# Attention kernel: 22 units' probabilities and B's values transposed as the rounded 32-bit type, one unit on

## The chip, the cores and the metric

The kernel runs on one NeuronCore of a Trainium2 chip. Its engines are TensorE (PE, with its weight load shown apart as PEld), VectorE (DVE), ScalarE (ACT), GpSimd (POOL) and SyncE (SP, which here only issues transfers). Each engine runs its own instructions in their order and waits on semaphores for the others. The metric is the device time of one execution in microseconds (us).

## The reference

One layer of an encoder on 1024 tokens of width 1024, in float32: a half-step FFN, then a mixer of two attentions, then a second half-step FFN. The mixer is what matters here:

```
u = RMSNorm(h)
qA,kA,vA,qB,kB,vB,gA,gB = split(u @ W_in)
yA = NeighbourhoodAttention2D(qA, kA, vA)        # 8 heads, 8x16 window, learned bias
yB = WindowedGQA(rope(qB), rope(kB), vB)         # 8 heads, 2 key heads, |i-j| <= 128, sink logit
h = h + (sigmoid(gA) * (yA @ W_A) + sigmoid(gB) * (yB @ W_B)) @ W_out
```

Both attentions are a softmax of scores over a band of keys, p = exp(s - max) / sum, and then p @ v.

## The kernel before

All large products are done on TensorE with both factors split in two tiles of the rounded 32-bit type (`fp32r` in the profile, `F32R` in the code): a high part, and the rest. Three matmuls (lines 149, 153 and 155, function `mm3`) make one product. The FFNs, the input projection and the branch products all go through `mm3`; the weights and activations are split by ACT (a cast, the high part) and DVE (a subtraction, the low part), mostly in `split`, lines 95 and 98.

Between them stands the attention stage, of some 230 us (from about 917 to 1160 us of the span). It handles 64 **units**, one after the other: a unit is a block of 128 queries with two heads. The first 32 are B's (`units_b`: eight blocks j, four pairs of heads each), the last 32 A's. A unit has nk = 3 blocks of 128 keys, in the first and the last block of queries only 2. Four functions make the steps of a unit, and the loop at the end of the stage lays them out as a pipeline, one unit entering per round n:

- `scores` (round n): on PE four matmuls into two PSUM tiles "d" (lines 1596 and 1597), then on DVE a custom operation that adds the mask or bias and keeps the running maximum (L1601), then on ACT the exponential with its sum (L1604). The result, the unscaled probabilities, lies in the tile `fa` in two places used in turn for two units of three, and in two `held` tiles (`hs` in the profile) for every third unit.
- `scale` (one round later): a reciprocal on DVE (L1610), and the scaling of one head on DVE (L1611) and of the other on ACT (L1612), in place.
- `turn` (two rounds later): nk transposes on PE for each of the two heads, 128 x 128 each, with the identity `ident`, into PSUM tiles "d" (L1620); then `split` of each (ACT L95, DVE L98) into tiles `ws`.
- `values` (three rounds later): on PE the products with the values (L1639 for B, L1634 for A), into a PSUM tile "g"; then the write, for B an ACT copy (L1539) and a DVE addition (L1540).

Between these steps the loop puts pieces of other PE work, the **filler**: first the products of the gates (`gate`, six matmuls of 512 columns in `mm3` for one piece, with ACT copies L1331 at the end of each gate), then B's branch products. The gates' weights come by SP transfers `ws<-wg_d` (L1228, 512 KB each, two per gate). A's operands come by POOL transfers (`prep_a`, L1303, L1306).

B's values are made earlier: `v_b` (L1153 to L1156) loads a row block of `z_d` by an SP transfer, and `turn_v` transposes it, eight transposes of 128 x 128 (L1163), before they are split.

What sets the order: outside the hand-written first stage, a list scheduler reorders the instructions of all engines by its own estimate of their times, so the order on each engine is not that of the code. The ring `raw` has four buffers of 512 KB, `ws` eight, the PSUM tags "d" and "g" four banks each.

Of the kernel before, what the change touches and what calls it, by code (L numbers as in the profile page):

```python
# [9 lines left out]

F32 = mybir.dt.float32
# [4 lines left out]
P = 128  # L16
# [15 lines left out]
def f32v(ap):  # L32
    return ap.bitcast(F32)
# [3 lines left out]
def trunk_kernel(ctx, tc, x, xt, n1, wg1, wu1, wd1, nm, win, rpb, sink, wa, wb, wout,  # L37
# [17 lines left out]
        uid[0] += 1  # L55
        return f"{s}_{uid[0]}"

    ident = const.tile([P, P], F32, name="ident")
    make_identity(nc, ident)
    nhalf4 = const.tile([P, 4], F32, name="nhalf")  # L60
    nc.gpsimd.memset(nhalf4, -0.5)
    nhalf = nhalf4[:, 0:1]
# [74 lines left out]
    def turned(xs):  # L137
        pts = []
        for half in range(2):
            pt = bank("d")  # L140
            for c in range(4):
                nc.tensor.transpose(pt[:, c * P:(c + 1) * P], xs[:, (half * 4 + c) * P:(half * 4 + c + 1) * P], ident)  # L142
            pts.append(pt.rearrange("p (c t) -> p c t", c=4))
        return pts

# [768 lines left out]
    def keep_busy(n):  # L914

        b = bank("g")
        for i in range(n):
            k = i % 4 * P
            nc.tensor.transpose(b[:, k:k + P], ident, ident)

    def first_stage():
        load, _, _, _, pieces, (multiply, finish), hand_over, load_early = hg
# [39 lines left out]
        def do(op, a):  # L962
# [13 lines left out]
            elif op == "eps":  # L976
                i = int(a[0])
                nc.vector.tensor_scalar(st[i][1], st[1][0] if i else mean[0].rearrange("p (k c) -> p k c", c=P)[:, :, 0], EPS, None, op0=ALU.add)
            elif op == "pow":
                i = int(a[0])  # L980
                nc.gpsimd.tensor_tensor(st[i][0], st[i][1], nhalf4, op=ALU.pow)
            elif op == "spread":
                i = int(a[0])
                r[i] = bank("d" if i else "g")
                for k in range(4):
                    nc.tensor.transpose(r[i][:, k * P:(k + 1) * P], st[i][0][:, k:k + 1].to_broadcast([P, P]), ident)
            elif op == "stat":
                t = int(a[0])
                nc.scalar.activation(toks[:, t - 4], toks[:, t - 4], AF.Square, scale=D ** -0.5,
                                     accum_out=st[1][0][:, t - 4:t - 3])  # L990
            elif op == "keep":
                rms["row"] = main.tile([P, 512], F32, tag="s1", bufs=1, name=nm_("s1"))
                nc.scalar.copy(rms["row"], r[0])
            elif a[0] == "X":
                c = int(a[1])
                h, l = [v[:, c, :] for v in rhs(B21)]
                if op == "hi":
                    nc.scalar.activation(h, block(c, 0, 1), AF.Copy, scale=n1c[:, 4 + c:5 + c])
                else:
                    nc.vector.scalar_tensor_tensor(out=l, in0=block(c, 0, 1), scalar=n1c[:, 4 + c:5 + c], in1=f32v(h),  # L1000
                                                   op0=ALU.mult, op1=ALU.subtract)
            elif op == "y":
                n, h, c = int(a[0][0]) - 1, int(a[0][1]) - 1, int(a[1])
                d, k = block(c, h, n), 4 * n + c
                nc.vector.scalar_tensor_tensor(out=d, in0=d, scalar=n1c[:, k:k + 1],
                                               in1=rms["row"] if (n, h) == (1, 0) else r[h], op0=ALU.mult, op1=ALU.mult)
            elif op == "t":
                c = int(a[1])
                y11, y21, y12, y22 = block(c, 0, 0), block(c, 0, 1), block(c, 1, 0), block(c, 1, 1)
                d, u, v = {"1": (y12, y12, y11), "2": (y22, y22, y12), "3": (y11, y22, y11), "4": (y21, y21, y22)}[a[0]]  # L1010
                nc.vector.tensor_tensor(d, u, v, op=ALU.subtract)
            elif a[0] in RIGHTS:
                c = int(a[1])
                src, g = block(c, *BLOCKS[a[0]]), RIGHTS[a[0]]
                if ar[g].dtype != F32R:
                    new_ar(g)
                h, l = [v[:, c, :] for v in rhs(RIGHTS[a[0]])]
                if op == "hi":
                    nc.scalar.copy(h, src)
                else:  # L1020
                    nc.vector.tensor_tensor(l, src, f32v(h), op=ALU.subtract)
            elif op == "load":
                i, m, half = [int(k) for k in a]
                load(i, m, half, {(0, 0): 4, (0, 1): 5, (1, 0): 6}[m, half])
            else:
                q = int(a[1]), a[0], int(a[2])
                if op == "mm":
                    if q not in mm:
                        mm[q] = multiply(*q)
                    drain(mm[q], 1)  # L1030
                elif op == "x":
                    drain(finish(*q), 1)
                else:
                    if q not in pc:
                        pc[q] = pieces(*q)
                    pc[q].pop(op)()
# [115 lines left out]

    def v_b():  # L1153
        mix["vb"] = [new_fx(k, F32R).rearrange("p (t d) -> p t d", t=NTT) for k in (0, 1)]
        mix["vr"] = xs4()
        pin(nc.sync.dma_start(mix["vr"], z_d[17 * P:18 * P, :]))  # L1156

    def turn_v():
        r = mix["vr"]
        for n in range(2):  # L1160
            pt = bank("g")
            for i in range(4):
                nc.tensor.transpose(pt[:, i * P:(i + 1) * P], r[:, (4 * n + i) * P:(4 * n + i + 1) * P], ident)  # L1163
            pt = pt.rearrange("p (b s d) -> p b s d", s=2, d=HD)
            for s in range(2):
                v = mix["vb"][s][:, 4 * n:4 * n + 4, :]
                split(v[:, :, :HD], v[:, :, HD:], pt[:, :, s, :])
# [410 lines left out]
                           bias=[bias_at(hp, s, edge) for s in range(2)], sink=None, write=write)  # L1578

    npair = [0]  # L1580

    def scores(un):
        j = un["j"]
# [2 lines left out]
        moff = (k0 - j + 1) * P  # L1586
        ext = 0 if un["sink"] is None else 1
        nmx, ssum, rc = small("nmx"), small("ssum"), small("rc")
        un.update(k0=k0, nk=k1 - k0, pr=[], ssum=ssum, rc=rc)
        third = npair[0] % 3 == 2  # L1590
        both = None if third else fa[:, 1536 + 2 * (npair[0] % 3) * (384 + ext):][:, :2 * (384 + ext)].rearrange("p (s k) -> p s k", s=2)
        if ext and not third:
# [1 line left out]
        for s in range(2):  # L1594
# [8 lines left out]
                                           accum_out=nmx[:, s:s + 1])  # L1603
            nc.scalar.activation(pr, pr, AF.Exp, scale=-1.0, bias=nmx[:, s:s + 1], accum_out=ssum[:, s:s + 1])  # L1604
            un["pr"].append(pr[:, ext:])
        npair[0] += 1

    def scale(un):
        rc = un["rc"]
        nc.vector.reciprocal(rc, un["ssum"])  # L1610
        nc.vector.tensor_scalar_mul(un["pr"][0], un["pr"][0], rc[:, 0:1])  # L1611
        nc.scalar.activation(un["pr"][1], un["pr"][1], AF.Copy, scale=rc[:, 1:2])  # L1612

    def turn(un):
        nk = un["nk"]
        un["p"] = [ws4()[:, :768].rearrange("p (k s t) -> p k s t", k=3, s=2) for _ in range(2)]
        for s in range(2):
            pt = bank("d")
            for i in range(nk):
                nc.tensor.transpose(pt[:, i * P:(i + 1) * P], un["pr"][s][:, i * P:(i + 1) * P], ident)  # L1620
            if len(un["v"]) == 2:
                dst = [un["p"][s][:, :nk, k, :] for k in range(2)]
            else:
# [34 lines left out]
    for n in range(1 << 30):  # L1658
# [9 lines left out]
        if prep:  # L1668
            drain(prep, 1)
        filling(n)  # L1670
        if len(pipe) > 2 and pipe[2] is not None:
            turn(pipe[2])
        if prep:
            drain(prep, 1)
        if n >= 26 and (n - 26) % 8 == 0 and n < 58:
# [8 lines left out]
        if n == 63:  # L1684
            form("P2", 0, mix["ya", 2][:, L])
        filling(n)
        if len(pipe) > 3 and pipe[3] is not None:
            values(pipe[3])
        pipe = pipe[:4]
        if not any(pipe):  # L1690
            break
    drain(fill)

# [247 lines left out]
```

## Time and profile before

| | us |
|---|---|
| median of 3 runs | 1912.72 (1911.67 to 1912.93) |
| the profiled execution | 1912.05 |
| its span | 1910.1 |
| PE busy in the span | 1901.1 (100%) |
| DVE busy | 1456.1 (76%) |
| ACT busy | 961.3 (50%) |

The profile is of one execution. The span runs from the first to the last instruction; the 1.95 us beside it lie around it. In the groups of instructions a row gives line, engine, operation, tiles, shape and count, then busy time, mean duration of one in ns, and the idle time of the engine just ahead of them. The duration of one matmul is longer than the distance to the next, because they are pipelined: the distance is read from the chain of waits, where a row gives start, time and what, and x6 means six in a row. A row with "issue" is time in which the engine waited for nothing that the profile shows.

### The profile page before, as it was taken

Reading aid. Unit: us, or ns where it says so; the run is one execution under the profiler, and the core shown is the slowest. Engines: PE = TensorE matmul, PEld = TensorE weight load, DVE = VectorE, ACT = ScalarE, POOL = GpSimd, SP = SyncE. Lnnn points to the kernel's source line nnn. Section 1 sums busy time; section 2 is a strip of 40 time slices with the busy share of each in tenths; the row PEclk is TensorE's granted clock in tenths of the full one; section 3 lists DMA queues with packets and bytes.
Section 4 is the critical chain, followed back from the end, with each engine's and each line's share of the span. In section 5 each row is a group of like instructions: output and inputs, shape, how many; then the busy total and the mean of one; then the engine's idle time right before and its main releaser. Section 6 shows DMA issues by size and latency. Waiting matters only on the chain.

```text
span 1910.1 us, 26150 instructions
## 1 busy us (share of the span) xinstructions
PE 1901.1 (100%) x9020; PEld 1595.1 (84%) x9020; DVE 1456.1 (76%) x2644; ACT 961.3 (50%) x1876; POOL 244.3 (13%) x453
## 2 busy tenths in 40 slices
PE   9999999999999999999999999999999999999998
PEld 8888888888888888898898888888888888888886
DVE  8988888868957788666888999789665566559664
ACT  7533545544446543444898885274333333344453
POOL 0011232210000112211112300010010001000011
PEclk9999999999999999999999999999999999999999
DMA  7256977887454367855647969653333323492341
GB/s 270 95 188 217 336 273 289 298 293 282 127 166 135 112 206 225 243 192 206 181 123 207 296 227 335 232 195 132 136 111 107 108 89 111 162 357 93 110 139 61
DMA packets 176963, 365.84 MB, mean 192 GB/s; under 512 B 17728, under 2 KB 75968, under 8 KB 176832
## 3 DMA queue, kind: packets, MB, share of 16 engines
q1 hardware_dynamic: 136784, 236.23, 37.6%
q0 software_dynamic: 39184, 126.90, 19.2%
q8 instruction: 71, 1.16, 0.3%
q10 hardware_dynamic: 864, 1.05, 0.2%
q14 instruction: 60, 0.49, 0.1%
HBM read 244.06 MB, written 121.83 MB: 192 GB/s over the span
## 4 chain that ended last, share of the span: by engine, by line
PE 96%; ACT 2%; DVE 1%; DMA 0%; issue 0%; SPq 0%; POOLq 0%; POOL 0%; DVEq 0%
PE g L149 18%; PE g L155 18%; PE g L153 18%; PE d L155 12%; PE d L149 12%; PE d L153 12%; PE d L1620 2%; PE g L1634 1%; PE d L1596 1%; PE d L1597 1%; PE g L1639 1%; PE d L142 1%; ACT fa L1604 0%; ACT ws L95 0%; DMA fx<-in_xt_dram 0%; DVE ws L98 0%
## 5 line engine op out<-in xcount | busy, mean ns | idle before, releaser
L149 PE MATMUL g<-ar,ws 128*128 128x512 f32 x1062 | 407.0, 393 | 0.2
L153 PE MATMUL g<-ar,ws 128*128 128x512 f32 x1062 | 403.8, 390 | 0.0
L155 PE MATMUL g<-ar,ws 128*128 128x512 f32 x1062 | 402.6, 390 | 0.0
L149 PE MATMUL d<-ar,ws 128*128 128x512 f32 x706 | 275.3, 390 | 0.0
L155 PE MATMUL d<-ar,ws 128*128 128x512 f32 x706 | 274.9, 389 | 0.1
L153 PE MATMUL d<-ar,ws 128*128 128x512 f32 x706 | 274.8, 389 | 0.0
L155 PEld LDWEIGHTS g<-ar,ws 128*128 128x128 f32 x1062 | 199.2, 188 | 41.8
L153 PEld LDWEIGHTS g<-ar,ws 128*128 128x128 f32 x1062 | 199.4, 188 | 40.7
L149 PEld LDWEIGHTS g<-ar,ws 128*128 128x128 f32 x1062 | 196.4, 188 | 37.1 <-ACT xs L1331 1.1
L334 DVE TENSOR_TENSOR ws<-raw,ws 128x512 fp32r<-128x512 f32 x216 | 147.6, 689 | 78.5 <-ACT ws L327 77.7
L327 ACT CAST ws<-raw 128x512 fp32r<-128x512 f32 x216 | 132.7, 620 | 143.1 <-PE g L155 61.2
L155 PEld LDWEIGHTS d<-ar,ws 128*128 128x128 f32 x706 | 132.5, 188 | 28.0 <-DVE ws L334 0.5
L153 PEld LDWEIGHTS d<-ar,ws 128*128 128x128 f32 x706 | 132.6, 188 | 27.7 <-DVE ar L1000 0.3
L149 PEld LDWEIGHTS d<-ar,ws 128*128 128x128 f32 x706 | 132.7, 188 | 27.1
L95 ACT CAST ws<-raw 128x512 fp32r<-128x512 f32 x88 | 54.9, 623 | 115.5 <-PE d L155 63.6
L98 DVE TENSOR_TENSOR ws<-raw,ws 128x512 fp32r<-128x512 f32 x88 | 60.5, 688 | 55.2 <-ACT ws L95 55.1
L95 ACT CAST ar<-raw 128x512 fp32r<-128x512 f32 (+1 forms) x80 | 52.1, 654 | 84.4 <-PE g L153 51.5
L446 POOL DMA_DIRECT2D hid<-fx x91 | 49.5, 544 | 343.2 <-DVE fx L506 221.6
L149 PE MATMUL g<-ws,ws 128*128 128x512 f32 x232 | 90.9, 392 | 0.0
L153 PE MATMUL g<-ws,ws 128*128 128x512 f32 x232 | 90.3, 389 | 0.0
L155 PE MATMUL g<-ws,ws 128*128 128x512 f32 x232 | 90.1, 390 | 0.0
L95 ACT CAST ws<-ar 128x512 fp32r<-128x512 f32 x104 | 64.3, 618 | 47.4 <-PE g L155 25.4
(382 smaller groups left out, 3878.7 us busy)
## 6 DMA issues: line engine op xcount, KB each, us to landing
raw<-hid SPq DMA_DIRECT2D x70, 512.0 KB
hid<-fx POOLq DMA_DIRECT2D x91, 256.0 KB, 2.9
ar<-in_ffn_w_down_dram SPq DMA_DIRECT2D x32, 512.0 KB
raw<-in_ffn_w_up_dram SPq DMA_DIRECT2D x31, 512.0 KB
wo_d<-made POOLq DMA_DIRECT2D x28, 512.0 KB, 4.6
raw<-in_ffn_w_gate_dram SPq DMA_DIRECT2D x27, 512.0 KB
hid<-fa POOLq DMA_DIRECT2D x51, 256.0 KB, 2.9
ar<-zs_d POOLq DMA_DIRECT2D x48, 256.0 KB, 9.3
```

Of the source, the lines that this page charges most:

```text
L95: hi = nc.scalar.copy(dst_hi, src)
L98: (eng or nc.vector).tensor_tensor(dst_lo, src, f32v(dst_hi), op=ALU.subtract)
L142: nc.tensor.transpose(pt[:, c * P:(c + 1) * P], xs[:, (half * 4 + c) * P:(half * 4 + c + 1) * P], ident)
L149: o = nc.tensor.matmul(b, lhs[0], r[0], start=first, stop=False, **kw)
L153: nc.tensor.matmul(b, lhs[0], r[1], start=False, stop=False, **kw)
L155: nc.tensor.matmul(b, lhs[1], r[0], start=False, stop=last, **kw)
L327: nc.scalar.copy(w[0][:, :512], a)
L334: nc.vector.tensor_tensor(w[0][:, 512:], a, f32v(w[0][:, :512]), op=ALU.subtract)
L446: nc.gpsimd.dma_start(hid[PRODUCTS.index(p), i], src)
L1596: nc.tensor.matmul(b[:, :nw], un["q"][s], un["kd"][s][:, k0 * P:k1 * P], start=True, stop=False)
L1597: nc.tensor.matmul(b[:, :nw], un["q"][s], un["kl"][s][:, k0 * P:k1 * P], start=False, stop=True)
L1620: nc.tensor.transpose(pt[:, i * P:(i + 1) * P], un["pr"][s][:, i * P:(i + 1) * P], ident)
```

## The change

For the first 22 units (all B's), after the scaling an SP transfer copies the scaled probabilities of both heads from `fa` or `hs` to a new tile `moved`, of the type F32R, in the ring `raw`. The transfer itself is of float32 to float32 (the tile's view as float32), so it casts nothing. For a unit in `fa` it is one transfer of 128 x 2 x 384 (384 KB; 256 KB with nk = 2), for a unit in `hs` two transfers, one per head. These 22 units' `turn` then transposes F32R tiles with an F32R identity into an F32R view of the PSUM tile, and comes a round later (place 3 of the pipeline in place of 2), as does their `values` (place 4 in place of 3). The other 42 units are handled as before. B's value rows (`vr`) are loaded into a tile declared F32R, and their eight transposes are of that type too. The identity is made by the same two POOL instructions, now in the kernel's own lines; all other transposes use its view as float32.

```diff
-    ident = const.tile([P, P], F32, name="ident")
-    make_identity(nc, ident)
+    ident = const.tile([P, P], F32R, name="ident")
+    nc.gpsimd.memset(f32v(ident), 0.0)
+    nc.gpsimd.affine_select(out=ident, in_=f32v(ident), compare_op=ALU.not_equal, fill=1.0, base=0, pattern=[[-1, P]],
+                            channel_multiplier=1)
...
-        mix["vr"] = xs4()
-        pin(nc.sync.dma_start(mix["vr"], z_d[17 * P:18 * P, :]))
+        mix["vr"] = main.tile([P, 1024], F32R, tag="xs", bufs=2, name=nm_("vr"))
+        pin(nc.sync.dma_start(f32v(mix["vr"]), z_d[17 * P:18 * P, :]))
...
-                nc.tensor.transpose(pt[:, i * P:(i + 1) * P], r[:, (4 * n + i) * P:(4 * n + i + 1) * P], ident)
+                nc.tensor.transpose(pt[:, i * P:(i + 1) * P].bitcast(F32R), r[:, (4 * n + i) * P:(4 * n + i + 1) * P], ident)
...
+    MOVED = 22
...
-        un.update(k0=k0, nk=k1 - k0, pr=[], ssum=ssum, rc=rc)
+        un.update(k0=k0, nk=k1 - k0, pr=[], ssum=ssum, rc=rc, moved=npair[0] < MOVED)
...
+        un["pair"] = un["pr"] if third else [both[:, :, ext:ext + nw]]
...
         nc.scalar.activation(un["pr"][1], un["pr"][1], AF.Copy, scale=rc[:, 1:2])
+        if un["moved"]:
+            nw = un["nk"] * P
+            x = main.tile([P, 1024], F32R, tag="raw", bufs=4, name=nm_("moved"))[:, :2 * nw].rearrange("p (s k) -> p s k", s=2)
+            if len(un["pair"]) == 1:
+                nc.sync.dma_start(f32v(x), un["pair"][0])
+            else:
+                for k in range(2):
+                    nc.sync.dma_start(f32v(x[:, k]), un["pair"][k])
+            un["pr"] = [x[:, k] for k in range(2)]
...
-                nc.tensor.transpose(pt[:, i * P:(i + 1) * P], un["pr"][s][:, i * P:(i + 1) * P], ident)
+                x = un["pr"][s][:, i * P:(i + 1) * P]
+                nc.tensor.transpose(pt[:, i * P:(i + 1) * P].bitcast(x.dtype), x, ident if un["moved"] else f32v(ident))
...
-        if len(pipe) > 2 and pipe[2] is not None:
-            turn(pipe[2])
+        for k, moved in ((3, True), (2, False)):
+            if len(pipe) > k and pipe[k] is not None and pipe[k]["moved"] == moved:
+                turn(pipe[k])
...
-        if len(pipe) > 3 and pipe[3] is not None:
-            values(pipe[3])
-        pipe = pipe[:4]
-        if not any(pipe):
+        for k, moved in ((4, True), (3, False)):
+            if len(pipe) > k and pipe[k] is not None and pipe[k]["moved"] == moved:
+                values(pipe[k])
+        pipe = pipe[:5]
+        if not any(pipe[:4]):
```

Where the scheduler puts it, on PE, in the middle of B's units. Before, between the scores of unit 11 and those of unit 12 (`d_8197`), stand six filler matmuls (the last two are shown), the transposes of unit 9 (from `fa`, two tiles "d") and the values of unit 8:

```order
L155 MATMUL g_7983<-ar_4840,ws_7766 128x512
L155 MATMUL g_7984<-ar_594,ws_7766 128x512
L1620 MATMUL d_8171<-ident,fa 128x128 x3
L1620 MATMUL d_8177<-ident,fa 128x128 x3
L1639 MATMUL g_8183<-ws_8121,fx_6579 128x256
L1639 MATMUL g_8183<-ws_8122,fx_6579 128x256
L1639 MATMUL g_8183<-ws_8121,fx_6579 128x256
L1639 MATMUL g_8183<-ws_8122,fx_6579 128x256
L1639 MATMUL g_8183<-ws_8121,fx_6579 128x256
L1639 MATMUL g_8183<-ws_8122,fx_6579 128x256
L1596 MATMUL d_8197<-ar_5218,ar_5219 128x384
```

and the same place after, again ahead of the scores of unit 12 (`d_8198`):

```order
L156 MATMUL g_7977<-ar_4840,ws_7758 128x512
L156 MATMUL g_7978<-ar_594,ws_7758 128x512
L1633 MATMUL d_8172<-ident,moved_8060 128x128 x3
L1633 MATMUL d_8178<-ident,moved_8060 128x128 x3
L1652 MATMUL g_8184<-ws_8121,fx_6580 128x256
L1652 MATMUL g_8184<-ws_8122,fx_6580 128x256
L1652 MATMUL g_8184<-ws_8121,fx_6580 128x256
L1652 MATMUL g_8184<-ws_8122,fx_6580 128x256
L1652 MATMUL g_8184<-ws_8121,fx_6580 128x256
L1652 MATMUL g_8184<-ws_8122,fx_6580 128x256
L1598 MATMUL d_8198<-ar_5218,ar_5219 128x384
```

The round holds as many instructions of each kind. Its transposes read `moved` and are those of unit 8, three units behind the scores of unit 11 that precede them, where before those of unit 9 stood here, two behind; the values are of unit 7 where they were of unit 8.

On SP, in the same stretch, after the change (`moved_8414` and `moved_8470` are units 15 and 16, `moved_8522` is unit 17 in its two halves, `ws<-wg_d` a gate's weights):

```order
L1620 DMA moved_8414<-fa 128x2x384
L1620 DMA moved_8470<-fa 128x2x384
L1229 DMA ws_8486<-wg_d 128x1024
L1229 DMA ws_8487<-wg_d 128x1024
L1623 DMA moved_8522<-hs_7682 128x384
L1623 DMA moved_8522<-hs_7683 128x384
L1620 DMA moved_8571<-fa 128x2x384
```

Before, the gates' loads of this stage stood in the queue with nothing between them; now the moved units' transfers stand between them, and each waits for what stands ahead of it.

On ACT, from one scaling to the next (units 17 and 18), before:

```order
L1612 ACTIVATE hs_7683<-hs_7683,rc_8440 128x384
L1539 COPY s_867_7677<-g_8480 64x256
L1604 ACTIVATE fa,ssum_8490<-fa,nmx_8489 128x385
L95 CAST ws_8506<-d_8508 128x3x128
L95 CAST ws_8506<-d_8514 128x3x128
L1604 ACTIVATE fa,ssum_8490<-fa,nmx_8489 128x385
L1612 ACTIVATE fa<-fa,rc_8491 128x384
```

and after:

```order
L1615 ACTIVATE hs_7683<-hs_7683,rc_8454 128x384
L1540 COPY s_867_7677<-g_8496 64x256
L96 CAST ws_8525<-d_8527 128x3x128
L1606 ACTIVATE fa,ssum_8506<-fa,nmx_8505 128x385
L96 CAST ws_8525<-d_8533 128x3x128
L1606 ACTIVATE fa,ssum_8506<-fa,nmx_8505 128x385
L1615 ACTIVATE fa<-fa,rc_8507 128x384
```

The same seven instructions stand between the two scalings (the casts now of an older unit); only one cast and one exponential have changed places.

More of the change, by code (lines that the diff above doesn't have):

```diff
@@ L7 @@
 from concourse import mybir
-from concourse.masks import make_identity
 from concourse._compat import with_exitstack
@@ L141, in turned @@
             for c in range(4):
-                nc.tensor.transpose(pt[:, c * P:(c + 1) * P], xs[:, (half * 4 + c) * P:(half * 4 + c + 1) * P], ident)
+                nc.tensor.transpose(pt[:, c * P:(c + 1) * P], xs[:, (half * 4 + c) * P:(half * 4 + c + 1) * P], f32v(ident))
             pts.append(pt.rearrange("p (c t) -> p c t", c=4))
@@ L918, in keep_busy @@
             k = i % 4 * P
-            nc.tensor.transpose(b[:, k:k + P], ident, ident)
+            nc.tensor.transpose(b[:, k:k + P], f32v(ident), f32v(ident))
     def first_stage():
@@ L985, in do @@
                 for k in range(4):
-                    nc.tensor.transpose(r[i][:, k * P:(k + 1) * P], st[i][0][:, k:k + 1].to_broadcast([P, P]), ident)
+                    nc.tensor.transpose(r[i][:, k * P:(k + 1) * P], st[i][0][:, k:k + 1].to_broadcast([P, P]), f32v(ident))
             elif op == "stat":
```

## The prediction

> **What bounds the kernel now.** I read the engines' busy shares first, then the chain of waits by engine, then the waits of PE alone.
>
> ```profile
> PE 1901.1 (100%) x9020; PEld 1595.1 (84%) x9020; DVE 1456.1 (76%) x2644; ACT 961.3 (50%) x1876; POOL 244.3 (13%) x453
> PE 96%; ACT 2%; DVE 1%; DMA 0%; issue 0%; SPq 0%; POOLq 0%; POOL 0%; DVEq 0%
> PE g L919 <- POOL ident masks.py:199: 1.5, 1, 1.5
> ```
>
> PE is busy all the span, it carries 96% of the chain, and the only wait of it that its view lists is one of 1.5 us at the start. So a microsecond of PE work that disappears is worth a microsecond, unless another engine is only just behind PE at that place. The groups of PE by shape, and the chain in order of time through one unit of B, give what the touched work costs.
>
> ```profile
> L1620 PE MATMUL d<-ident,fa 128*128 128x128 f32 x236 | 33.9, 273 | 0.1
> L1639 PE MATMUL g<-ws,fx 128*128 128x256 f32 x176 | 27.4, 289 | 0.0
> L1620 PE MATMUL d<-ident,hs 128*128 128x128 f32 x116 | 16.6, 272 | 0.0
> L1163 PE MATMUL g<-ident,xs 128*128 128x128 f32 x8 | 1.0, 272 | 0.0
> ```
>
> ```profile
> 941.94 0.66 PE d L1620 x6
> 942.60 0.72 PE g L1639 x6
> 943.31 0.18 PE d L1596
> ...
> 944.01 0.47 PE g L149 x2
> ...
> 945.40 0.65 PE d L1620 x6
> ```
>
> A unit takes 945.40 - 941.94 = 3.46 us, and six float32 transposes are 0.65 to 0.66 of it: 0.109 us each. In the rounded type a matmul of 256 columns takes 0.72 / 6 = 0.120, one of 384 columns (944.01 - 943.31) / 4 = 0.175, since four score matmuls of that width stand between these rows, one of 512 columns 0.47 / 2 = 0.235.
>
> **How near the other engines are.** The 2% of ACT and 1% of DVE in the chain are not spread over the span. In order of time they stand here:
>
> ```profile
> 962.25 0.24 PE g L155
> ...
> 962.52 1.07 ACT xs L1331 x2
> ...
> 973.47 0.71 ACT hs L1604 x2
> ...
> 974.20 0.49 ACT ws L95
> ...
> 974.71 1.02 DVE ws L98 x2
> 975.74 0.13 DVE rc L1610
> ...
> 975.90 0.62 ACT hs L1612
> ...
> 976.55 0.37 ACT s L1539
> ...
> 976.93 0.71 ACT fa L1604 x2
> ...
> 993.73 0.47 DVE ws L98
> 994.21 0.04 issue
> 994.25 0.55 PE d L1620 x3
> ```
>
> From 962.5 to 994.2 us, about nine units, no step of the chain is PE's. One turn of it is an exponential on ACT, a cast, two subtractions on DVE, the reciprocal, the scaling on ACT and the copy of the written values: from 973.47 to 976.93, 3.46 us. That is PE's own pace. In these nine units PE and the pair ACT and DVE are both at the limit.
>
> **The change, part by part.** *The transposes.* The units moved are 4 with nk = 2 and 18 with nk = 3: 4 x 4 + 18 x 6 = 124 transposes, and 8 more of B's values, so 132. No row shows a transpose of the rounded type, nor a matmul of that type with 128 columns. The step from 384 to 256 columns is 0.175 - 0.120 = 0.055; one step further gives an estimate of 0.065. From below the bound is half of the float32 transpose, 0.055, if that goes over its columns twice and the new one once. From above, the nearest row of the type is the 256 columns' 0.120, if something that does not shrink with the columns (the weight load) holds the pace; farther off stands a plain float32 product of 128 columns:
>
> ```profile
> 13.52 2.05 PE g L974 x16
> L1620 PEld LDWEIGHTS d<-ident,fa 128*128 128x128 f32 x236 | 28.6, 140 | 5.1 <-DVE ws L98 0.3
> L1639 PEld LDWEIGHTS g<-ws,fx 128*128 128x128 f32 x176 | 24.1, 189 | 1.4
> ```
>
> Eight such products (two records each) take 2.05, 0.256 each. I take 0.065: the two records of a plain float32 product beside the one of a transpose, and the even steps between widths, say that time goes with passes over the columns. Saved on PE: 132 x (0.109 - 0.065) = 5.8 us.
>
> One rule of the Trainium skill speaks against this. Its page "TensorE: Matmul & The Clock Gate", section "LDWEIGHTS (loading the stationary operand)", has a weight load take its 128 columns at 1.2 per ns, an estimate of 107 ns, whatever the matmul behind it. By that the 109 ns of a transpose are its weight load's, and nothing is saved. The trace neither refutes nor shows it: no pair of load and matmul comes closer than 109 ns, and the load's own record is 140 ns before float32 transposes but 189 ns before matmuls of the rounded type. This is the second rival below.
>
> *What of it can be collected.* Units 0 to 11 lie ahead of 962.5, where the chain is PE's: 4 x 4 + 8 x 6 = 64 transposes, 2.8 us. The 60 of units 12 to 21, 2.6 us, lie under the turn of ACT and DVE. In the new order ACT still has copy, two casts, two exponentials and the scaling from one scaling to the next; only two have changed places, and the reciprocal still waits for the same things. So I count nothing there; at best all. The eight transposes of B's values, 0.35 us, count in full: there the chain is PE's. Together 3.2 us, bounds 0.3 and 5.8 (7.1 at 0.055).
>
> *The transfers.* 22 units issue 29 (seven in `hs` have two), 384 KB a unit. They cost PE nothing if they land ahead of the transpose. SP's own landings are not shown; POOL's are:
>
> ```profile
> hid<-fx POOLq DMA_DIRECT2D x91, 256.0 KB, 2.9
> v_d<-v POOLq DMA_DIRECT2D x8, 512.0 KB, 3.2
> raw<-y_d POOLq DMA_DIRECT2D x4, 512.0 KB, 9.7
> 923.92 73.78 SPq L1228 DMA_DIRECT2D ws<-wg_d  x8
> 956.75 0.62 ACT L1612 ACTIVATE hs<-hs,rc 128x384 f32<-128x384 f32 x1
> 959.10 0.82 PE L1620 MATMUL d<-ident,hs 128*128 128x128 f32 x6
> ```
>
> So 2.9 to 3.2 us where the queue is quiet, and up to 9.7 among other loads. The cover: before, the scaling of unit 11 ends at 957.37 and its transposes start at 959.10, 1.7 us later, one of the short ones. The round that is added gives 3.4 more, 5.1 in all, so a quiet transfer has 1.9 us to spare. Without the added round it would be late by 1.4 us in such units. Not all are quiet. The gates' loads (L1228), which before waited in the queue for 73.8 us with nobody behind them, now have moved units behind them: behind three pairs of loads, a transfer waits for a `ws` buffer to come free and then shares the engines with 1 MB. PE stops at the late transpose; values, scores and filler stand behind it, and ACT's casts wait for it. I put 0.5 us on each of the three, 1.5 us, bounds 0 and 3 x (9.7 - 5.1) = 13.8.
>
> *The rest.* The longer pipeline costs PE no idle time: in round 2, where no transpose comes, the order has filler. The two extra issues per unit in `hs`, the identity (the same two POOL instructions) and the DVE order are off the path; if the filler ran short, the added round would cost one unit's ACT and DVE time once, about 3 us.
>
> *Sum*: -3.2 + 1.5 = -1.7 us on the profiled execution's 1912.05 (span 1910.1 and 1.95 around it), so 1910.35. The median of the runs is 0.67 above that execution: **1911.0 us**. Its own range is 1908 to 1913: the transfers at nothing (-1.5), the later units half collected (-1.3), or two more short waits (+2).
>
> **The rivals.**
>
> - *All of it is collected.* The transposes run at 0.055 to 0.065 and ACT and DVE gain as well, because casts find their PSUM tile ready sooner and one more unit of slack lies between scaling and cast. For it: ACT is not full, 8.86 of 10 us in the row below, and its records overlap. Against it: nine units with no PE in the chain.
>
> ```profile
> 950.00:960.00 10.00, 10.00 (x65) 9.06 (x65) 9.10 (x31) 8.86 (x25) 1.78 (x3) 1.00 0.37 79
> 980.00:990.00 10.00, 10.00 (x66) 9.16 (x65) 9.15 (x31) 9.39 (x25) 1.79 (x3) 1.00 0.35 80
> ```
>
>   In these two rows (PE, PEld, DVE, ACT, POOL) PE is full, DVE 9.1 and ACT 8.9 to 9.4 of 10 us. Price: 1912.7 - 5.8 to 7.1, with no late transfer: 1906.3.
> - *The type changes nothing*: the transpose stays at 0.109 to 0.120, by the weight load or because the array moves four bytes in two passes either way. Then 0 to +1.4 us on PE and +1.5 of late transfers: 1914.2, from 1912.7 to 1916. The load's longer record speaks for it, the even steps between widths against it.
> - *Slower, by the width*: the type loses its pace in matmuls as narrow as 128 columns, and a transpose costs what a plain float32 product does, 0.256. Place: lines 1633 and 1164. Price: 132 x 0.147 = 19.4, and 1.5: 1933.6. It decides from 0.109 on, each further 0.01 costs 1.3 us. For it: nothing in the trace is that narrow. Against it: 256 columns show no sign of it.
> - *Slower, by the queue*: the transfers behind the gates' loads land like `raw<-y_d`, three stops of 4.6 us: -3.2 + 13.8, so 1923.3. It decides from a landing of 5.1 us on. Against it: POOL's other loads of this size land in 3.2.
>
> **How the numbers follow.** Forecast 0.42, all collected 0.18, type without effect 0.24, slower by the width 0.08, by the queue 0.08. About 0.2%, 3.8 us, is what a measurement of this kernel can tell from no change: faster means below 1908.9, slower above 1916.5. Faster: 0.15 of the all-collected and 0.05 of the forecast, 0.20. Slower: 0.15 of the last two and 0.01 of the type without effect, 0.16. Same: 0.64. The range 1906.0 to 1916.0 holds the forecast, nearly all of the type without effect (0.24) and 0.14 of the all-collected: 0.80.
>
> **What would show it.** In the profile after: the distance between the transposes of line 1633 in the chain (0.065 right; 0.109 or above, the rivals); the pace of units 12 to 21, 3.4 us or more if ACT and DVE hold it, 3.2 if not; waits of PE for the transfers, if any, behind `ws<-wg_d` loads. The prediction is wrong if PE waits for `moved` in most units, or if the pace falls to 3.2 us in all of them.

## The result

The changed kernel is slower: 1919.67 us, the median of five runs (1918.79 to 1926.14), against 1912.72 (five runs, 1911.67 to 1913.94). The ratio is 1.0045, with a 95% interval of 1.0027 to 1.0063: 7 us by the medians and 8.6 by the ratio, where 1.7 less than before was forecast. The ratio is the recorded one; the medians alone would give 1.0036, and two of the five runs took over 1923 us. The ratios below are the recorded ones as well. The profiled execution took 1918.93 us, 6.9 more than that of before; its span is 6.8 us longer.

The page of the changed kernel begins so, with its busy shares and its chain by engine:

```profile
span 1916.9 us, 26260 instructions
...
PE 1901.6 (99%) x9020; PEld 1590.5 (83%) x9020; DVE 1454.6 (76%) x2644; ACT 960.3 (50%) x1876; POOL 243.6 (13%) x453
...
PE 95%; ACT 2%; DMA 2%; DVE 1%; issue 1%; POOL 0%; SPq 0%; POOLq 0%; ACTq 0%; DVEq 0%
```

DMA now has 2% of the chain, where it had none. The windows show where PE stands still: B's units of the attention stage. First before, then after (PE, PEld, DVE, ACT, POOL, then clock, DMA share, GB/s):

```profile
917.00:967.00 50.00, 50.00 (x309) 44.86 (x309) 42.98 (x153) 42.92 (x121) 7.62 (x14) 1.00 0.50 144
967.00:1017.00 50.00, 49.93 (x319) 45.25 (x319) 43.15 (x146) 44.17 (x116) 8.77 (x15) 1.00 0.44 122
```

```profile
917.00:967.00 50.00, 46.56 (x281) 39.81 (x280) 38.75 (x142) 39.82 (x109) 6.32 (x11) 1.00 0.72 207
967.00:1017.00 50.00, 47.61 (x299) 41.56 (x298) 40.58 (x136) 41.60 (x110) 7.58 (x13) 1.00 0.64 183
```

In these 100 us PE is idle 5.8 us and issues 580 matmuls where it issued 628, and ACT and DVE are busy less too. All three wait; none has become the bound by its own work. The list of waits in B's units says for what:

```profile
DVE fa L1595 <- DMA moved<-fa: 11.6, 7, 2.8
...
PE d L1633 <- DMA moved<-fa: 2.7, 2, 1.4
...
PE d L1633 <- DVE ws L99: 1.8, 3, 0.9
...
DVE hs L1603 <- DMA moved<-hs: 0.6, 1, 0.6
```

PE's own waits for late transfers, which the prediction had looked for, are 2.7 of its 5.8 us. But DVE waits 12.2 us for transfers, at L1595 above all: the copy of the sink's column into the place in `fa` that the transfer of an older unit is still reading. One such wait in DVE's order (the first row is an earlier maximum, of the unit whose transfer is waited for), then PE's next transposes, then the same place in the chain:

```profile
961.19 0.61 DVE L1603 CUSTOM_DVE_ANT_0 fa<-d,masks,nsk 128x384 f32<-128x384 f32 x1
...
969.78 0.60 DVE L1603 CUSTOM_DVE_ANT_0 fa<-d,masks,nsk 128x384 f32<-128x384 f32 x1
970.32 0.08 DVE L1603 DVE_READ_ACCUMULATOR2_ANT nmx<- 128x1 f32 x1
973.21 0.17 DVE L1595 COPY fa<-nsk 128x2 f32<-128x2 f32 x1 [2.81 <-DMA moved<-fa]
973.28 0.55 DVE L99 TENSOR_TENSOR ws<-d,ws 128x384 fp32r<-128x384 f32 x1
973.75 0.61 DVE L1603 CUSTOM_DVE_ANT_0 fa<-d,masks,nsk 128x384 f32<-128x384 f32 x1
```

```profile
973.89 0.98 PE L1633 MATMUL d<-ident,moved 128*128 128x128 f32 x6 [0.90 <-DVE ws L99]
```

```profile
967.95 5.24 DMA moved<-fa
973.18 0.02 issue
973.21 0.17 DVE fa L1595
973.37 0.06 DVE ws L99
973.43 0.32 issue
973.75 0.61 DVE fa L1603
974.36 0.02 DVE nmx L1603
974.38 0.04 issue
974.42 0.45 PE d L1633 x3
974.87 0.53 PE g L150 x2
```

DVE stops for 2.81 us at a copy of 0.17 us, and behind it in its queue stand a subtraction and the score maximum of the unit that the copy belongs to, both of which read a PSUM tile "d". PE stands still for 0.90 us until the subtraction is done; in the chain, the second three of its six transposes (974.42) follow the maximum. The transfer took 5.24 us from issue to release.

### The profile page after: what moved, and what is told of

Read it like the earlier page. It is cut to its first block, busy times and chain, and to the rows that moved or that the text cites. A ratio compares the mean times of both kernels' runs of the same rounds, so it can differ in the third digit from the quotient of the medians.

```text
span 1916.9 us, 26260 instructions
## 1 busy us (share of the span) xinstructions
PE 1901.6 (99%) x9020; PEld 1590.5 (83%) x9020; DVE 1454.6 (76%) x2644; ACT 960.3 (50%) x1876; POOL 243.6 (13%) x453
## 4 chain that ended last, share of the span: by engine, by line
PE 95%; ACT 2%; DMA 2%; DVE 1%; issue 1%; POOL 0%; SPq 0%; POOLq 0%; ACTq 0%; DVEq 0%
PE g L150 18%; PE g L156 18%; PE g L154 17%; PE d L150 12%; PE d L156 12%; PE d L154 12%; PE d L1633 1%; DMA moved<-fa 1%; PE g L1647 1%; PE d L1598 1%; PE d L1599 1%; PE d L143 1%; PE g L1652 1%; ACT fa L1606 0%; DMA fx<-in_xt_dram 0%
```

## The experiments

All were timed in five rounds against the kernel before, whose median was 1912.4 to 1912.9 in each set. The first theory: the transfers hold the places of the probabilities, DVE runs into them, and PE starves behind DVE. The rivals: PE's own waits for late data; the load of the transfers on the DMA engines; the longer pipeline.

**What the type gives.** In the first run the change is kept, and only the type of the 124 transposes is undone (`x` is the slice that is turned):

```diff
-  nc.tensor.transpose(pt[...].bitcast(x.dtype), x, ident if un["moved"] else f32v(ident))
+  nc.tensor.transpose(pt[...], f32v(x) if un["moved"] else x, f32v(ident))
```

> The changed kernel with its transfers and the turn one unit on, but the 124 transposes of the moved units as float32 (the moved tile and the identity are read as float32); B's values stay of the rounded type. In the changed kernel six transposes of the rounded type take 0.45 to 0.47 us (0.075 each) where float32 ones took 0.65 to 0.66 (0.109), so the type gives 124 x 0.034 = 4.2 us of PE's time back. Theory (the type's gain is real and added to by about 11 us of new stalls, whatever the type): 1919.7 + 4.2 = 1923.9. Rival (the stalls set the pace of the stage and swallow whatever PE saves): 1919.7, same as the changed kernel.

Measured: 1924.51 us, ratio 1.0066 (1.0054 to 1.0078), 4.8 above the changed kernel's median, 4.0 by the ratios, whose intervals overlap. So the stalls do not seem to swallow the type's gain; they come on top of it.

In the second the type stands alone, without transfers, and with the turn and the values back in their old places:

```diff
+  x = main.tile([P, 1024], F32R, tag="raw", ...)[...]; dst = [x[:, k] for k in range(2)]
-  nc.vector.tensor_scalar_mul(un["pr"][0], un["pr"][0], rc[:, 0:1])
+  nc.vector.tensor_scalar_mul(dst[0], un["pr"][0], rc[:, 0:1])
-  nc.scalar.activation(un["pr"][1], un["pr"][1], AF.Copy, scale=rc[:, 1:2])
+  nc.scalar.activation(dst[1], un["pr"][1], AF.Copy, scale=rc[:, 1:2])
```

> The type without transfer and without delay: for the first 22 units the scaling of DVE and of ACT writes a tile of the rounded type in the ring raw, which is transposed as in the kernel before. This rounds the probabilities of these units to the type, so the low part that is split off afterwards is lost. All 124 transposes at 0.075: if ACT and DVE give way and all is collected, 1912.7 - 4.2 - 0.3 (the values' eight) = 1908.2. By the prediction's own step (units 12 to 21 are held by ACT and DVE and collect nothing): 64 x 0.034 + 0.3 = 2.5, 1910.2.

Measured: 1910.71 us, ratio 0.9992 (0.9983 to 1.0000). That is about 2 us by the medians and 1.5 by the ratio, less than either sum. The chain of this run, over one unit that the prediction counted as PE's, and over one that it gave to ACT and DVE:

```profile
941.95 0.47 PE d L1630 x6
942.42 0.79 PE g L1649 x6
...
945.29 0.47 PE d L1630 x6
...
968.92 0.46 PE d L1630 x6
969.38 0.54 PE g L150 x2
...
972.24 0.47 PE d L1630 x6
972.71 0.53 PE g L150 x2
```

Six transposes take 0.47 us, 0.078 each, not 0.065; and the matmuls right behind them take longer than before: 0.79 where six of the values took 0.72, 0.53 or 0.54 where two of 512 columns took 0.47. So 0.06 to 0.07 of the 0.18 is given back at once, and a unit falls from 3.46 to 3.34 us (945.29 - 941.95), 0.02 a transpose. It falls as far behind 962.5: 972.24 - 968.92 = 3.32. There the chain is now PE's as well, up to 985.8; from there to 992.7, about two units, it still goes through ACT and DVE. Over the whole stage this trace gains 1.6 us: the first unit that is not moved turns at 995.99, where it was 997.61. The first six units gain nothing (941.95 against 941.94 at the seventh).

**The delay.** The first attempt took the change's pipeline and left the transfers out:

```diff
-        if un["moved"]:
-            nw = un["nk"] * P
...
-            un["pr"] = [x[:, k] for k in range(2)]
```

> Only the longer pipeline: the first 22 units are turned and multiplied with the values one unit later, straight from fa and hs as float32, no transfers. Theory (the transfers make the stalls, the delay none): 1912.7, within 2 us. Rival (the longer pipeline itself costs: DVE's place in the order, buffers held longer): up to 1912.7 + 11 = 1924.

Measured: 1922.35 us, ratio 1.0056 (1.0043 to 1.0069). It looks like the rival, but the kernel is not what the expectation takes it for. With three places, unit n's turn now comes behind the scores of unit n+3, which use the same place: it turns what that unit has written, so that these units' results are lost, and PE has to wait for the newer unit's exponential. PEld's waits in B's units show it:

```profile
PEld d L1624 <- ACT fa L1606: 3.4, 7, 1.3
```

So it says nothing of the delay. The clean one takes the kernel with the type alone, where a place is free as soon as the scaling has read it, and turns one unit on:

```diff
-        for k, moved in ((2, True), (2, False)):
+        for k, moved in ((3, True), (2, False)):
             if len(pipe) > k and pipe[k] is not None and pipe[k]["moved"] == moved:
                 turn(pipe[k])
...
-        for k, moved in ((3, True), (3, False)):
+        for k, moved in ((4, True), (3, False)):
             if len(pipe) > k and pipe[k] is not None and pipe[k]["moved"] == moved:
                 values(pipe[k])
```

> The kernel with the type alone (scaling writes the rounded tile in the ring raw, 1910.71) with the turn and the values of the first 22 units one unit later, as in the change; no transfers, and the place in fa is free as soon as the scaling has read it, so that the longer pipeline holds nothing but ring buffers. Theory (the transfers make the loss, the delay none): 1910.7, within 1.5 us. Rival (the longer pipeline itself costs): between 1913 and 1919.7.

Measured: 1910.94 us, ratio 0.9991 (0.9983 to 1.0000). The longer pipeline costs nothing.

**The transfers, one burden at a time.** All of these start from the type alone. First, transfers that nobody reads but that hold the place:

```diff
+  y = main.tile([P, 1024], F32R, tag="raw", bufs=4, name=nm_("spare"))[...]
+  if len(un["pair"]) == 1:
+      nc.sync.dma_start(f32v(y), un["pair"][0])
+  else:
+      for k in range(2):
+          nc.sync.dma_start(f32v(y[:, k]), un["pair"][k])
```

> The kernel with the type alone (turned where the kernel before turns), and beside it the 29 transfers of the change from fa and hs into a spare buffer of raw that nobody reads: same sizes, same queue, and the place in fa or hs is held until they have read it, but PE waits for none of them. Theory (DVE's stop at the next writing of the place is the loss): DVE waits at the sink's copies as in the changed kernel, 7 or so times, and the time is 1916 to 1920. Rival (PE's own waits for late data are the loss): 1910.7 to 1912.

Measured: 1921.88 us, ratio 1.0044 (1.0031 to 1.0057): the whole loss of the change, with no data that anybody waits for, and a little above the range expected. DVE's waits, and the windows of B's units:

```profile
DVE fa L1595 <- DMA spare<-fa: 10.2, 6, 3.2
```

```profile
917.00:967.00 50.00, 45.60 (x273) 39.65 (x272) 37.87 (x135) 37.81 (x105) 6.17 (x11) 0.97 0.76 226
967.00:1017.00 50.00, 48.00 (x293) 42.11 (x292) 39.60 (x137) 41.67 (x109) 6.50 (x11) 0.97 0.63 182
```

PE is idle there for 6.4 us, where the change has 5.8, and the clock of 0.97 takes some 3 us more. The traced execution is the longest of the five, 1927.9 us. It has a further stop of PE of 4.3 us at 1109, in A's units, where DVE waits at L1565 for the write `y_d<-fa`; the change's trace has none there. What makes that write late was not tested.

The next was to leave only the load, by letting the same transfers read the buffer in `raw`:

```diff
-  nc.sync.dma_start(f32v(y), un["pair"][0])
+  nc.sync.dma_start(f32v(y), f32v(x))
```

> As the run before, but the 29 transfers read the rounded tile in raw, not fa or hs, so that they hold no place that DVE writes again; only the load on SP's queue and on the DMA engines is left, and the two more allocations in raw per unit. Theory: 1910.7 to 1912. Rival (the load of the transfers on the DMA engines, and what they delay there, is the loss): 1915 to 1920.

Measured: 1921.08 us, ratio 1.0041 (1.0026 to 1.0056). Taken alone this is the rival's number, but the waits show that this kernel, too, holds a buffer short: with two allocations per unit in a ring of four, the scaling two units on writes what the transfer still reads.

```profile
DVE moved L1619 <- DMA spare<-moved: 6.4, 4, 2.5
...
ACT moved L1620 <- DMA spare<-moved: 4.9, 4, 1.9
```

So the load was tried again with transfers that hold nothing that is wanted soon:

```diff
             split(dst[0], dst[1], pt[:, :nk * P].rearrange("p (k t) -> p k t", k=nk))
+        if un["moved"]:
+            y, src = un["old"], fa[:, :2 * nk * P].rearrange("p (s k) -> p s k", s=2)
+            nc.sync.dma_start(f32v(y), src)
```

This stands at the end of `turn`; `old` is the buffer in `raw` that has just been turned, and for the units of `hs` there are again two transfers.

> The kernel with the type alone, and 29 transfers of the change's sizes on SP's queue that nobody's work waits for: after a unit's turn they write A's bias (which nothing writes at that time) over the unit's spent buffer in raw, which is wanted again only two units later. Here the load on SP's queue and on the DMA engines stands alone, without a place or a buffer held short. Theory (held buffers are the loss): 1910.7 to 1912.5. Rival (the load itself is the loss: it delays POOL's loads, the gates' weights or the writes, and they delay the engines): 1916 to 1921.

Measured: 1910.94 us, ratio 0.9993 (0.9984 to 1.0002). Here the transfers from `fa` have a source without the gap between the heads and go as 128 packets of 3072 B; with the change's 256 of 1536 B:

```diff
-  fa[:, :2 * nk * P].rearrange("p (s k) -> p s k", s=2)
+  fa[:, :2 * nk * P + 2].rearrange("p (s k) -> p s k", s=2)[:, :, :nk * P]
```

> idle_late with the change's 256 packets of 1536 B. Theory (the load costs nothing): 1910.7 to 1912, as idle_late's 1910.9. Rival (the load of so many packets costs): 1914 or more.

Measured: 1910.54 us, ratio 0.9995 (0.9986 to 1.0004). The load costs nothing, with either kind of packet; nothing waits for a transfer of `moved` in B's units of these traces.

Then late data without a held place, in both kinds of packets:

```diff
         un["pr"] = dst
+        if un["moved"]:
+            x, src = un["x"], fa[:, :2 * un["nk"] * P].rearrange("p (s k) -> p s k", s=2)
+            nc.sync.dma_start(f32v(x), src)
```

This is in `scale` of the clean delay's kernel; `x` is the tile that the scaling has just written.

> PE waits for the transfers, DVE does not: the scaling writes its rounded tile in raw and so frees the place in fa at once; then the transfer of the change (same sizes, same queue, started when the scaling has ended, turned one unit on) writes A's bias over that tile, and PE turns what the transfer has written (the probabilities of these units are left out of the result). Theory (the held place is the main loss, late data a small one): 1910.9 for the kernel without transfers, plus PE's direct waits of some 1 to 3 us: 1912 to 1914. Rival (late data to PE are the main loss): 1917 to 1920.

> data_only with the source read with the change's gap between the heads, so that a transfer from fa has the change's 256 packets of 1536 B (128 of 3072 B in data_only; PE again turns A's bias in place of these units' probabilities). Theory (late data are a small part whatever the packets): 1912 to 1914.5, as data_only's 1913.4. Rival (the packets make the data late, and that is what wide_from_start has left): 1916 to 1918.

Measured: 1913.44 us, ratio 1.0009 (0.9998 to 1.0020), and 1911.73, ratio 1.0001 (0.9993 to 1.0010). Against the same kernel without transfers (1910.94, ratio 0.9991) that is 1 to 3 us by the medians and 2 to 3.5 by the ratios. It doesn't show that a late transfer is cheap: in the two traces PE waits 0.6 us and nothing at all for `moved`, so where no place is held the data are seldom late. Five of the twelve executions of the first took 1914.5 to 1919.5, the others 1909.9 to 1912.3; none of the longer ones was traced.

**Relieving the place.** In the change itself the sink's copy can go, since DVE meets the place there first:

```diff
-        if ext and not third:
+        if ext and not third and npair[0] >= 25:
```

> The changed kernel without the copies of the sink's column into fa for the first 25 units (left out: these units' probabilities then take a stale number as the sink's term). DVE then meets the held place only at the score maxima of that unit, which stand later in its order. Theory (DVE's early stop at that copy is most of the loss): 1912 to 1915, with waits left at the maxima. Rival (the place is late for the maxima as well, or PE's own waits are the loss): 1918 to 1920.

Measured: 1919.65 us, ratio 1.0033 (1.0021 to 1.0045). This went against the first form of the theory, in which the early copy was most of the loss: DVE now waits at the maxima, which write the same place:

```profile
DVE fa L1603 <- DMA moved<-fa: 8.4, 5, 2.2
```

The place itself is late, not only the copy early. A fourth place should then help, and this was tried first with the copies kept:

```diff
+        wide = npair[0] < 24
-        third = npair[0] % 3 == 2
+        third = npair[0] % 4 == 3 if wide else npair[0] % 3 == 2
-        both = None if third else fa[:, 1536 + 2 * (npair[0] % 3) * (384 + ext):]...
+        both = None if third else fa[:, 1536 + 2 * (npair[0] % (4 if wide else 3)) * (384 + ext):]...
```

> The changed kernel with one place more for the probabilities of the first 24 units: three places in fa and the pair in hs, used in turn for four units instead of three, so that a place is written again one unit (3.4 us) later. Theory (DVE stops at the writing of the sink column into fa until the transfer has read the old probabilities, 7 waits of 11.6 us in all, and the maxima, scalings and subtractions queued behind it come late to PE): these waits go, PE keeps only its direct waits for transfers, some 3 us: 1911 to 1913. Rival (PE's own waits for late transfers and the load of the transfers on the DMA engines are the loss): 1917 to 1920.

Measured: 1923.55 us, ratio 1.0065 (1.0045 to 1.0085): no relief, and above even the rival's range. The scheduler put some of the copies earlier still, and the first use of the new place met an older transfer, of the stage before:

```profile
DVE fa L1596 <- DMA moved<-fa: 5.2, 4, 2.1
...
DVE fa L1596 <- DMA g_d<-fa: 3.7, 1, 3.7
```

The waits for `moved` are halved, and a new one of 3.7 us has come in their stead; PE also stops for 3.4 us at 1108 in A's units, as in idle_from_fa behind the write `y_d<-fa`. Without the copies, and on the kernel whose transfers only hold the place, the test is clean (the same four places as above, on the run idle_from_fa):

> The run idle_from_fa (transfers that nobody reads, which hold the place in fa; 1921.9), with the place relieved: three places in fa and the pair in hs in turn for units 0 to 23, and no copies of the sink's column into fa for these units (left out). Theory: a place is wanted again 3.4 us later, so DVE waits for no transfer in most units: 1911 to 1914. Rival (something else in those transfers is the loss): 1919 to 1923.

Measured: 1912.66 us, ratio 1.0001 (0.9993 to 1.0010), against 1.0044 with three places. One unit more between two uses of a place, with the copies gone, takes away four fifths of what the transfers cost ((1.0044 - 1.0001) / (1.0044 - 0.9992)). On the change itself, without the copies, with the fourth place from unit 3 on, from unit 0 on, and from unit 3 with the turn a further unit later:

```diff
+        wide = 3 <= npair[0] < 26; place = (npair[0] - 3) % 4 if wide else npair[0] % 3
...
-        for k, moved in ((3, True), (2, False)):
+        for k, moved in ((4, True), (2, False)):
```

The last two lines belong to the third of these runs alone (its values follow at place 5).

> The changed kernel with three places in fa and the pair in hs in turn for units 3 to 25 (a place is written again four units on, not three), and without the copies of the sink's column into fa for these units (left out), which the scheduler else puts early in DVE's order. Theory (the place held by the transfer is the main loss): DVE waits for no transfer; PE's own waits for late data (2.7 us in the changed kernel) stay: 1912 to 1914.5. Rival (data that come late to PE are the loss): 1918 or more.

> The changed kernel with four places in turn from unit 0 on (units 0 to 23), and without the copies of the sink's column into fa for these units (left out). In wide_no_sink, which began at unit 3, DVE still waited twice, for 3.4 us in all, at the first units. Theory: those two waits go as well: 1915.7 - 3.4 = 1912.3, within 1.5. Rival (PE's late data and the gates' loads ahead in the queue set what is left): 1915 to 1916.

> As the run before, and turn and values of the moved units one unit later still (two units later than in the kernel before), so that a transfer has 3.3 us more to land. Theory: neither DVE nor PE waits for a transfer, and the time is that of the type alone, 1910.7 to 1912. Rival (the load of the transfers costs by itself): 1915 or more.

Measured: 1915.73 us, ratio 1.0023 (1.0011 to 1.0035); 1917.49, ratio 1.0028 (1.0017 to 1.0040); 1918.90, ratio 1.0029 (1.0017 to 1.0041). All are better than three places without the copies by the ratio's middle, though the intervals overlap, and none reaches what was expected (1910.7 to 1914.5). In the traces DVE's waits for `moved` are 3.4 us in the first and gone in the second. In the third they are 5.7 us; the longest comes where the gates' weights and POOL's loads moved beside the transfer, which took 9.2 us from its issue:

```profile
957.71 0.62 DVE L1605 CUSTOM_DVE_ANT_0 fa<-d,masks,nsk 128x384 f32<-128x384 f32 x1 [3.16 <-DMA moved<-fa]
```

The second shows one long wait of PE for late data, and what follows it. PE's instructions in order of time, then the windows (the clock stands behind POOL):

```profile
928.51 0.63 PE L154 MATMUL g<-ar,ws 128*128 128x512 f32 x2
932.31 0.72 PE L1634 MATMUL d<-ident,moved 128*128 128x128 f32 x4 [3.17 <-DMA moved<-fa]
932.83 1.18 PE L156 MATMUL g<-ar,ws 128*128 128x512 f32 x2
```

```profile
928.00:932.00 4.00, 1.13 (x6) 0.70 (x4) 1.83 (x6) 0.40 (x2) 0.00 (x0) 0.96 1.12 213
932.00:936.00 4.00, 3.69 (x15) 3.43 (x16) 1.21 (x3) 2.21 (x7) 0.00 (x0) 0.50 0.10 32
936.00:940.00 4.00, 4.00 (x19) 3.52 (x18) 2.23 (x10) 2.72 (x8) 0.00 (x0) 0.68 0.00 0
```

After 3.17 us of standing still the granted clock is 0.50 and then 0.68: 4 x 0.50 + 4 x 0.32 = 3.3 us more are lost, as much as the wait itself. (In this trace, too, PE stops in A's units behind `y_d<-fa`, for 1.6 us.)

**A faster version.** The type alone was also given to all 64 units, and to B's 32 (`MOVED = 32`):

```diff
-    MOVED = 22
+    MOVED = 64
```

> The type alone for all 64 units, 352 transposes instead of 124 (their probabilities are rounded by the scaling). In the run with 124 the pace of a full unit fell from 3.46 to 3.34 us, 0.02 a transpose. If A's units are bound by PE as well, 1912.6 - 352 x 0.02 - 0.2 = 1905.4; if A's stage is held by DVE or by transfers, 1909 to 1910.7.

> The type alone (scaling writes the rounded tile in raw, no transfers, turned as in the kernel before) for all 32 units of B, 176 transposes instead of 124. Theory (PE sets the pace in all of B's units, 0.02 us a transpose): 1912.5 - 176 x 0.02 - 0.2 = 1908.8. Rival (ACT and DVE hold the last ten units, or the ring raw is wanted by other loads there): 1910.7 to 1912.

Measured: 1911.70 us, ratio 0.9996 (0.9987 to 1.0005), and 1909.77, ratio 0.9984 (0.9975 to 0.9993). With all of B's units the kernel is 3 us faster than before, between the two times expected and 0.9 below the median of the type alone, at the price of probabilities rounded to the type. In A's units the gain does not show: with all 64, PE is idle for 4.3 us between 1067 and 1167 us, with the first 22 units alone for 0.03. What makes it wait there was not tested.

## Why the prediction was wrong

**The step that failed** is the cover of the transfers, with the sentence that the DVE order is "off the path". The prediction asked who reads the moved data and by when, and found 5.1 us. It did not ask who wants the old place again. Before, a place in `fa` or `hs` was free when its unit had been turned, two rounds behind its scores. Now it is free when the transfer has landed, and with three places it is wanted three units on; the maximum, the exponential, the scaling, SP's issue, the transfer and the next maximum make a ring that must go round in three units, some 10 us. In the wait shown above, with 5.24 us for the transfer, 12.0 us pass from the unit's first maximum (961.19) to the release of its place (973.19). DVE stops, and with it casts, maxima and scalings of other units, so that the next transfer also starts later. Shown: holding the place alone costs as much as the change (1.0044), a fourth place without the sink's copies gives four fifths of that back (1.0001), and neither delay nor load costs anything. On the change itself the same relief gives back half at best (1.0045 to 1.0023). Of the signs that the prediction had named against itself, waits of PE for `moved` in most units did not come: there are two.

**The transfers' price** was near. Quiet, 2.4 to 2.5 us pass from issue to the last packet in the trace after; beside other loads 3 to 5.7, with 2.9 to 3.2 and up to 9.7 foreseen. PE's own waits are 2.7 us where 1.5 were put. The rival "slower, by the queue", at 1923.3, had the right sign, and with 10.6 us against 7 nearly the size, but the wrong engine: it saw PE stop behind the gates' loads, and by the runs the weight lies on DVE.

**The transposes** were mis-sized: 0.065 was taken, 0.078 is what they take among themselves, and 0.089 with what the matmuls behind them give back. So 124 would save 2.5 us at that rate, not 124 x 0.044 = 5.5; the trace gains 1.6. Read one by one in that trace, the first two distances between starts in a row of six are 0.058 to 0.069 and the others mostly 0.08 to 0.09, though the weight load's own record is 140 ns as before. It looks as if something, the weight load perhaps, ran ahead by one or two and then set the pace; this was not tested. The rule of the Trainium skill that was set against the estimate (page "TensorE: Matmul & The Clock Gate", section "LDWEIGHTS (loading the stationary operand)", an estimate of 107 ns for 128 columns) pointed the right way, but its figure is not what this trace shows: transposes with a load each come 0.078 us apart.

**What can be collected** failed as well, the other way: units 12 to 21 were counted at nothing, and with the type alone their pace fell like that of the others, to 3.32 to 3.35 us, even where the chain still went through ACT and DVE. So these engines were not full there; that the chain went through them because all waits were just met is the likely reading, not a tested one. The rows with 8.9 to 9.4 busy in 10 us, which the prediction quoted for the rival, were the better reading. The two errors cancel in part, by luck: 3.2 us were put, about 2 measured.

**What stays open.** With the place relieved, the change still takes 3 to 5 us more by the ratio than data_only and data_only_256 (1.0023 to 1.0029 against 1.0001 to 1.0009). The clock after a long wait is part of it in two of the three traces (wide_from_start and wide_and_later), and the stop in A's units in one; why the first units' data come later there than in data_only, where the transfers start at about the same point, was not settled.

## What to carry to other kernels

A transfer that is put between a producer and a consumer has two deadlines: the data must land before the reader, and the source must be read before its next writer. Count the second as a ring, with all buffers of the source, and look at what stands in the writer's in-order queue behind it. A chain that runs through an engine is no proof that the engine is full: look at its busy time too.

## What the runs showed of the hardware

A stop of PE can be paid for twice, once as the wait and once as a lower clock behind it. With float32 transposes (f32_moved) a wait of 1.85 us, 2.25 between matmul starts, is followed by 0.70 and 0.88 in the next two windows of 4 us, and the 3.17 us above by 0.50 and 0.68. The length of the stop does not decide it alone: in the same trace of f32_moved a longer wait, of 2.23 us, leaves the clock at 1.00, and so do gaps of up to 1.8 us between starts in the changed kernel's. The two places in f32_moved, the longer wait first:

```profile
930.59 0.41 PE L1633 MATMUL d<-ident,moved 128*128 128x128 f32 x2 [2.23 <-DMA moved<-fa]
```

```profile
928.00:932.00 4.00, 1.77 (x12) 1.22 (x11) 1.45 (x6) 1.79 (x8) 0.00 (x0) 1.00 0.69 143
932.00:936.00 4.00, 4.00 (x26) 3.47 (x24) 3.82 (x15) 3.95 (x14) 0.00 (x0) 1.00 0.19 66
```

```profile
949.38 1.40 PE L1633 MATMUL d<-ident,moved 128*128 128x128 f32 x6 [1.85 <-DVE ws L99]
```

```profile
944.00:948.00 4.00, 3.54 (x22) 2.81 (x20) 1.24 (x7) 2.60 (x8) 0.75 (x2) 1.00 1.03 297
948.00:952.00 4.00, 2.62 (x13) 2.52 (x14) 3.75 (x14) 2.23 (x6) 0.00 (x0) 0.70 0.66 219
952.00:956.00 4.00, 4.00 (x24) 3.69 (x23) 3.04 (x11) 3.22 (x11) 0.00 (x0) 0.88 0.97 358
```

The page "TensorE: Matmul & The Clock Gate" of the Trainium skill, section "What's actually happening", has the clock fall to half after an idle window of about 3.4 us and rise again after a busy one. The half agrees with the 0.50 above. So does the length of the low clock: counted as time at half clock, 0.70 and 0.88 make 3.4 us, and 0.50 and 0.68 make 6.6, about twice that. The idle time does not agree: here the clock fell after a wait of 1.85 us, and stayed after one of 2.23. The wide spread of the runs that stall (1918.8 to 1926.1 for the change, 1909.6 to 1910.1 for type_32) would follow if the clock falls in some executions and not in others. The two longest of the change have a mean clock of 0.998 and the others 0.999, and the traced one of idle_from_fa, 1927.9 us long, has 0.996. That fits, but no longer execution of the change was traced.
